# The low parts of 64 weight units of an encoder block, by an accumulating transfer in place of a subtraction

## The chip, the cores and the metric

The kernel runs on one core of a Trainium2 chip. The metric is the device time of one execution in microseconds (us). Before the change it is 1455.4 us, the median of three runs (1455.38 to 1455.77). The engines are named as in the profile: PE (TensorE, matrix products), PEld (its weight loads), DVE (VectorE), ACT (ScalarE), POOL (GpSimd) and SP (SyncE, which issues most DMAs).

## What is computed

One layer of a bidirectional encoder on 256 tokens of width 2048, in float32. Cut to what matters:

```python
h = rms_norm(x, attn_norm)
proj = h @ w_in                                  # q, k, v of two attention branches, and two gates
ya = windowed_gqa(qa, ka, va, table, sink)       # banded attention
yb = dilated_attention(qb, kb, vb, table)        # three dilations, merged
merged = sigmoid(ga) * (ya @ w_branch_a) + sigmoid(gb) * (yb @ w_branch_b)
x = x + merged @ w_out
hf = rms_norm(x, ffn_norm)
g = dwconv_centred(hf @ w_ffn_gate, conv_w, conv_b)
x = x + (gelu(g) * (hf @ w_ffn_up)) @ w_ffn_down # inner width 5632
x = x + sigmoid(rms_norm(x, ple_norm) @ w_ple_gate) * (p @ w_ple_proj)
out = rms_norm(x, final_norm)
```

## The kernel before

**Split products.** A float32 matrix product is made of three products of operands in the rounded type float32r. Each operand is split into a high part, its rounding, and a low part, the rest. `thirds` (L405 to L410) multiplies high by high (L408), high by low of the weights (L409) and low by high (L410), all into the same PSUM bank. The stages with 128-column moving weights do the same in `unit_blocks` (L335 to L358).

**Weights.** All weights come from HBM as 258 pieces of 128 partitions by 2048 columns, in the order in which they are used. SP loads a piece into one of three buffers `raw` (`load`, L250 to L258). `produce` (L285 to L311) makes one unit at a time, a part of a piece with at most 1024 columns: ACT writes the high part `hi` (L305), DVE writes the low part `lo` as the piece less `hi` (L306). Plain units (kind `n`) go to a ring of 6 buffers (tiles `uh`, `ul`), units of sums to a ring of 2 (`vh`, `vl`). Before a unit of piece p is made, the loads up to piece p + 2 are issued; a load must wait until the buffer's last readers have ended. When PE has used a unit for the last time, `drop` frees its place and `pump` makes what fits.

**Stages and pieces.** Stage A holds the projections for attention, with attention woven in. Behind it come the gates (B0 to B3), each followed by its share of the two branch products (ba, bb), then the output projection (D0, D1), and twice an up-projection (E0, E1) with two stages of the down-projection (F00, F01; F10, F11), the small projection pp, and the last gate G0, G2, G3. In the quad stages B, D, F and G0 (`quad_stage`) a piece holds two by two blocks of 512 columns. A piece of kind `S` or `Z` is multiplied in seven products by sums of blocks, each of three matmuls: it has two plain units and two units of sums, and DVE makes those sums in `raw` first (L282, L283, L295 to L297). A piece of kind `s` is multiplied in eight plain products and has two plain units. The branch products and G2, G3 have pieces of kind `w`, also two plain units and eight products (`wide_stage`). The kinds alternate in B and D (`SsSsSsSs`; B0 begins with four `s`), and in F (`ZZsZsZsZsZs`; `ZsZsZsZsZss` in the second half). For pieces of kind `Z` two of the sums are made ahead, in E0 and E1, by loads and stores on POOL's DMA queue (`sum_ahead`, L268 and L275, 52 of each), and loaded with the piece.

**Order.** Work beside the products is hung onto product numbers by `at` and done by `run_due`: gathers, norms, turns of rows into columns (L939, with roundings at L512, L513) and the ends of a stage (L890 to L894, L971 to L990, L1005, L1007). `keep` marks instructions that stay in program order. The rest is ordered on each engine by the framework's planner, so ACT's order can differ from the program's; each engine then takes its instructions strictly in turn.

Of the kernel before, what the change touches and what calls it, by code (L numbers as in the profile page):

```python
# [10 lines left out]
F32 = mybir.dt.float32  # L11
FR = mybir.dt.float32r
AF = mybir.ActivationFunctionType
ALU = mybir.AluOpType
# [149 lines left out]
_PIECES, _STAGES = _pieces()  # L164
# [3 lines left out]
def _unit_list():  # L168

    units, of = [], []  # L170
    for p, (kind, _) in enumerate(_PIECES):
        if p == 0:
            cuts = [("n", a * P, b * P) for a, b in ((0, 1), (1, 4), (4, 7), (7, 11), (11, PIECE))]
        elif kind == "Z":
            cuts = [("n", WIDE, 2 * WIDE), ("n", 2 * WIDE, 4 * WIDE), ("T21", 0, 2 * WIDE), ("T03", 2 * WIDE, 4 * WIDE)]
        elif kind == "S":
            cuts = [("n", 0, WIDE), ("n", 2 * WIDE, 4 * WIDE), ("T13", 0, 2 * WIDE), ("T24", 2 * WIDE, 4 * WIDE)]
        else:
            cuts = [("n", 0, 2 * WIDE), ("n", 2 * WIDE, 4 * WIDE)]
        of.append(list(range(len(units), len(units) + len(cuts))))  # L180
        units += [(p, *cut) for cut in cuts]
    return units, of


_UNITS, _UNITS_OF = _unit_list()
_FBLOCKS = [(u, o) for p, (kind, _) in enumerate(_PIECES) if kind == "f" for u in _UNITS_OF[p]
            for o in range((_UNITS[u][3] - _UNITS[u][2]) // P)]
_LAST_OF = {u: o for u, o in _FBLOCKS}
# [5 lines left out]
def _encoder(ctx: ExitStack, tc, xt, pt, xrow, cols, gainrow, table, onehot, mask, ident_in, wts, out):  # L194
    nc = tc.nc
# [12 lines left out]
    def bank(which, *shape):  # L208

        if which in RING:  # L210
            n = turns.get(which, 0)
            turns[which] = n + 1
            which = RING[which][n % len(RING[which])]
        else:
            which = BANK[which]
        return ps.tile(list(shape) or [P, 2 * T], F32, name="bank", tag="b%d" % which, bufs=1)
# [33 lines left out]
    def load(r, a=0, b=PIECE):  # L250
        if a == 0:
            raws[r] = wpool.tile([P, PIECE * P], F32, name="raw", bufs=3)
        if _PIECES[r][0] == "Z":
            nc.sync.dma_start(raws[r][:, WIDE:], wts[r][:, WIDE:])
            nc.sync.dma_start(raws[r][:, :WIDE], ahead.pop(r))
        else:
            nc.sync.dma_start(raws[r][:, a * P:b * P], wts[r][:, a * P:b * P])
        state["raw"] = r + 1  # L258
# [20 lines left out]
    def sums_of_weights(raw):  # L279

        q = [raw[:, i * WIDE:(i + 1) * WIDE] for i in range(4)]
        nc.vector.tensor_tensor(q[1], q[0], q[1], op=ALU.subtract)  # L282
        nc.vector.tensor_tensor(raw[:, 2 * WIDE:], raw[:, 2 * WIDE:], view(q[0], 0, (0, 2), (1, WIDE)), op=ALU.subtract)  # L283

    def produce():  # L285

        u = state["unit"]
        p, kind, a, b = _UNITS[u]
        while state["raw"] < min(p + 3, _NPIECES):
            load(state["raw"])  # L290
        raw = raws[p]
        ring = "u" if kind == "n" else "v"
        if kind == "T13":
            q = [raw[:, i * WIDE:(i + 1) * WIDE] for i in range(4)]
            nc.vector.tensor_tensor(raw[:, :2 * WIDE], raw[:, WIDE:3 * WIDE], raw[:, :2 * WIDE], op=ALU.subtract)  # L295
            nc.vector.tensor_tensor(q[2], q[2], q[0], op=ALU.subtract)
            nc.vector.tensor_tensor(q[3], q[3], q[2], op=ALU.subtract)  # L297
        behind = _PIECES[p][0] == "Z" == _PIECES[p - 1][0]
        if kind == "T21" and not behind:
            sums_of_weights(raw)  # L300
        src = raw[:, a:b]
        pool = wpool if ring == "u" else held["tok"]
        hi = pool.tile([P, b - a], FR, name=ring + "h", bufs=RINGS[ring])
        lo = pool.tile([P, b - a], FR, name=ring + "l", bufs=RINGS[ring])
        nc.scalar.activation(hi, src, AF.Copy)  # L305
        nc.vector.tensor_tensor(lo, src, hi.bitcast(F32), op=ALU.subtract)  # L306
        if behind and u == _UNITS_OF[p][1]:
            sums_of_weights(raw)
        made[u] = (hi, lo)
        state["unit"] = u + 1  # L310
        state[ring] -= 1  # L311

    def pump():
        while not state["early"] and state["unit"] < len(_UNITS):
            p, kind = _UNITS[state["unit"]][:2]
            if state["u" if kind == "n" else "v"] <= 0 or kind != "n" and "tok" not in held:
                break
            produce()

    def weights(u):  # L320
        while state["unit"] <= u:
            produce()
        return made[u]
# [167 lines left out]
    keep = tc.keep_in_program_order  # L491
# [148 lines left out]
    for step in order:  # L640
        if len(step) == 3:
            produce()
        else:
            for k in range(*step):
                gained(hs[:, k, :], x[:, k, :], gain(0, k))
            ready = step[1]
        while state["at"] < min(FIRST * ready, _EARLY[state["unit"]]):
            k, e = divmod(state["at"], FIRST)
            block(firsts[e], hs[:, k, :], k == 0, k == KC - 1)
        while 4 * done + 9 < state["at"] // FIRST:  # L650
            square(done)
            done += 1
# [16 lines left out]
    b = bank("misc", NH, 2 * T)  # L669
# [470 lines left out]
    for half in range(2):  # L1140
# [3 lines left out]
        stage = "E%d" % half  # L1144
# [87 lines left out]
    for t in range(2):  # L1232
        for h in range(2):
            cols = slice(3 * WIDE + h * T, 3 * WIDE + (h + 1) * T)
            u, r = c[t][:, WIDE + h * T:WIDE + (h + 1) * T], xr[:, t, cols]
# [72 lines left out]
```

## Time and profile before

The profiled execution has a span of 1453.7 us from its first instruction to its last; the median of the runs, 1455.4 us, lies 1.7 us above it. The mean granted TensorE clock is 0.997 of full speed.

| | |
|---|---|
| SP's loads of weights waiting for `ul` of DVE (L257) | 718.4 us in 148 waits, the longest 10.1 |
| ACT's high parts `uh` (L305) waiting for PE's L410 | 106.5 us in 78 waits |
| ACT's high parts `uh` waiting for a load of `raw` | 41.5 us in 35 waits |
| DVE's low parts `ul` (L306) waiting for ACT's `uh` | 65.9 us in 61 waits |
| DMA, main queue (SP): bytes, share of 16 engines | 280.46 MB, 53.1% |
| HBM read, written | 299.94 MB, 8.95 MB |

A row of the timeline gives the start and the duration of an instruction in us from the span's start, its engine, line and operation, what it writes and reads, and in brackets how long the engine was idle before it and what released it. Neighbours of one form are merged (x3). A matmul of 512 columns is shown with 0.39 us, though the next one starts earlier: matmuls overlap.

### The profile page before, as it was taken

The page shows a single profiled execution, that of the slowest core. Times are in us where ns is not written, and L with a number is a line of the kernel's source. Part 1 is how long each engine was busy: PE and PEld are TensorE (multiplying, and loading weights), DVE is VectorE, ACT ScalarE, POOL GpSimd, SP SyncE. Part 2 cuts the span into 40 slices and gives each one's busy share as a digit, 9 for nine tenths or more (in the row PEclk, how much of TensorE's full clock was granted, in tenths as well). Part 3 has the DMA queues.
Part 4 walks back from the last instruction along what each step waited for, and adds up shares of the span by engine and source line. Part 5 has one row for each costly group of instructions (what it writes and reads, how often), then busy time and mean ns, then how long its engine had stood idle before and what let it go on. Part 6 is the DMA issues. An engine that isn't in the chain of part 4 may idle for free.

```text
span 1453.7 us, 19747 instructions
## 1 busy us (share of the span) xinstructions
PE 1442.7 (99%) x7470; PEld 1234.0 (85%) x7470; DVE 1220.8 (84%) x1730; ACT 829.6 (57%) x1148; POOL 73.8 (5%) x113
## 2 busy tenths in 40 slices
PE   9999999999999999999999999999999999999997
PEld 8888888888888888888888888888888888888885
DVE  7677665679998989989877999997878799998994
ACT  7455544546555656566545566465545466555753
POOL 0000000000000000000221100000121200000000
PEclk9999999999999999999999999999999999999998
DMA  9753445435456456465767655566776765556462
GB/s 330 252 209 146 155 167 175 172 143 203 189 190 231 180 210 239 178 253 203 277 238 267 241 208 198 189 248 227 263 275 243 271 236 213 197 194 233 173 236 82
DMA packets 58522, 310.17 MB, mean 213 GB/s; under 512 B 7028, under 2 KB 12020, under 8 KB 29500
## 3 DMA queue, kind: packets, MB, share of 16 engines
q1 hardware_dynamic: 49388, 280.46, 53.1%
q0 software_dynamic: 8320, 27.27, 5.2%
q8 instruction: 58, 0.95, 0.3%
q10 hardware_dynamic: 720, 1.19, 0.2%
q14 instruction: 36, 0.29, 0.1%
HBM read 299.94 MB, written 8.95 MB: 212 GB/s over the span
## 4 chain that ended last, share of the span: by engine, by line
PE 98%; DMA 0%; issue 0%; DVE 0%; ACT 0%; SPq 0%; POOLq 0%; POOL 0%; DVEq 0%
PE bank L351 29%; PE bank L358 15%; PE bank L408 15%; PE bank L409 14%; PE bank L410 14%; PE bank L397 2%; PE bank L399 2%; PE bank L398 2%; PE bank L335 2%; PE bank L336 1%; PE bank L939 1%; PE bank L755 0%; PE bank L703 0%; PE bank L702 0%; PE bank L701 0%; DMA raw<-in_wts 0%
## 5 line engine op out<-in xcount | busy, mean ns | idle before, releaser
L305 ACT ACTIVATE uh<-raw 128x1024 fp32r<-128x1024 f32 (+2 forms) x519 | 518.1, 1010 | 297.0 <-PE bank L410 106.5
L306 DVE TENSOR_TENSOR ul<-raw,uh 128x1024 fp32r<-128x1024 f32 (+2 forms) x519 | 594.4, 1164 | 96.5 <-ACT uh L305 65.9
L351 PE MATMUL bank<-hf,uh 128*128 128x512 f32 x1408 | 336.3, 391 | 0.0
L351 PEld LDWEIGHTS bank<-hf,uh 128*128 128x128 f32 x1408 | 258.9, 188 | 50.1
L358 PEld LDWEIGHTS bank<-hf,ul 128*128 128x128 f32 x1408 | 180.4, 191 | 6.7
L358 PE MATMUL bank<-hf,ul 128*128 128x256 f32 x1408 | 182.8, 283 | 0.0
L305 ACT ACTIVATE vh<-raw 128x1024 fp32r<-128x1024 f32 x96 | 101.1, 1058 | 59.8 <-DVE raw L282 27.0
L306 DVE TENSOR_TENSOR vl<-raw,vh 128x1024 fp32r<-128x1024 f32 x96 | 116.3, 1220 | 1.1
L351 PE MATMUL bank<-hs,uh 128*128 128x512 f32 x432 | 103.6, 392 | 0.0
L351 PEld LDWEIGHTS bank<-hs,uh 128*128 128x128 f32 x432 | 79.5, 188 | 15.6
L410 PE MATMUL bank<-uh,act 128*128 128x512 f32 x218 | 84.9, 390 | 0.0
L409 PE MATMUL bank<-ul,act 128*128 128x512 f32 x218 | 84.8, 389 | 0.0
L408 PE MATMUL bank<-uh,act 128*128 128x512 f32 x218 | 84.6, 390 | 0.0
L496 ACT ACTIVATE t<-bank 128x256 f32<-128x256 f32 x122 | 45.3, 374 | 59.8 <-PE bank L358 48.7
L408 PE MATMUL bank<-uh,hs 128*128 128x512 f32 x172 | 67.4, 392 | 0.0
L410 PE MATMUL bank<-uh,hs 128*128 128x512 f32 x172 | 67.2, 391 | 0.0
L409 PE MATMUL bank<-ul,hs 128*128 128x512 f32 x172 | 67.0, 389 | 0.0
L1084 ACT ACTIVATE gw<-gw,cl 128x256 f32<-128x256 f32 x44 | 24.0, 594 | 72.2 <-DVE gw L1081 71.9
L271 DVE TENSOR_TENSOR ahead<-ahead 128x256 f32<-128x256 f32 x52 | 21.9, 422 | 46.8 <-DMA ahead<-in_wts 46.8
L268 POOL DMA_DIRECT2D ahead<-in_wts x52 | 39.0, 750 | 375.7 <-DMA ahead<-ahead 207.0
L358 PE MATMUL bank<-hs,ul 128*128 128x256 f32 x432 | 56.6, 284 | 0.0
L358 PEld LDWEIGHTS bank<-hs,ul 128*128 128x128 f32 x432 | 54.5, 191 | 1.0
(266 smaller groups left out, 2423.8 us busy)
## 6 DMA issues: line engine op xcount, KB each, us to landing
raw<-in_wts SPq DMA_DIRECT2D x225, 1024.0 KB, 4.9
ahead<-in_wts POOLq DMA_DIRECT2D x52, 384.0 KB, 5.2
raw<-in_wts SPq DMA_DIRECT2D x26, 768.0 KB, 5.1
ahead<-ahead POOLq DMA_DIRECT2D x52, 128.0 KB, 4.4
raw<-ahead SPq DMA_DIRECT2D x26, 256.0 KB, 4.9
raw<-in_wts SPq DMA_DIRECT2D x12, 512.0 KB, 7.0
xr<-in_xrow SPq DMA_DIRECT2D x4, 512.0 KB, 8.4
x<-in_xt SPq DMA_DIRECT2D x13, 128.0 KB, 6.0
```

Source lines behind the costliest of these rows:

```text
L268: keep(nc.gpsimd.dma_start(q, wts[p][:, :3 * WIDE].rearrange("p (q c) -> p q c", c=WIDE)[:, :, cols]))
L305: nc.scalar.activation(hi, src, AF.Copy)
L306: nc.vector.tensor_tensor(lo, src, hi.bitcast(F32), op=ALU.subtract)
L335: nc.tensor.matmul(acc, hi[:, w], m, start=first, stop=False, skip_group_check=True)
L351: nc.tensor.matmul(acc, weights(u)[0][:, o * P:(o + 1) * P], m, start=first, stop=False, skip_group_check=True)
L358: nc.tensor.matmul(acc[:, T:], weights(u)[1][:, o * P:(o + 1) * P], m[:, :T], start=False, stop=last, skip_group_check=True)
L397: nc.tensor.matmul(acc[:, :n * P], xh, hi, start=(k == 0), stop=False)
L398: nc.tensor.matmul(acc[:, :n * P], xh, lo, start=False, stop=False)
L408: nc.tensor.matmul(acc, sh, wh, start=first, stop=False)
L409: nc.tensor.matmul(acc, sh, wl, start=False, stop=False)
L410: nc.tensor.matmul(acc, sl, wh, start=False, stop=last)
L496: keep(nc.scalar.activation(t, acc[:, T:], AF.Copy, scale=scale))
```

## The change

For 64 plain units, the second unit of each piece of kind `s` or `w` in the stages B, ba, bb, D, F and G0 (the set `_MOVED`), the low part is no longer made by DVE. ACT first writes the negated rounding of the unit into `lo`, then the rounding into `hi`, and POOL's queue issues a DMA that adds the piece to `lo`, from `raw` in SBUF to `lo` in SBUF, 128 partitions by 1024 elements. `lo` then holds the piece less its rounding, as before, though not rounded again. The DMAs stay in program order. All other units are made as before.

```diff
+_MOVED = {_UNITS_OF[p][1] for stage in _STAGES if stage[0] in "BbDFG" and stage not in ("G2", "G3")
+          for p in _STAGES[stage] if _PIECES[p][0] in 'sw'}
...
         hi = pool.tile([P, b - a], FR, name=ring + "h", bufs=RINGS[ring])
         lo = pool.tile([P, b - a], FR, name=ring + "l", bufs=RINGS[ring])
-        nc.scalar.activation(hi, src, AF.Copy)
-        nc.vector.tensor_tensor(lo, src, hi.bitcast(F32), op=ALU.subtract)
+        if u in _MOVED:
+            nc.scalar.activation(lo, src, AF.Copy, scale=-1.0)
+            nc.scalar.activation(hi, src, AF.Copy)
+            keep(nc.gpsimd.dma_start(lo, src if _PIECES[p][0] in "sw" else wts[p][:, a:b], accum_op=ALU.add))
+        else:
+            nc.scalar.activation(hi, src, AF.Copy)
+            nc.vector.tensor_tensor(lo, src, hi.bitcast(F32), op=ALU.subtract)
         if behind and u == _UNITS_OF[p][1]:
             sums_of_weights(raw)
```

## The prediction

> **What bounds the kernel now.** I read the page first: the busy shares and the chain that ended last.
>
> ```profile
> span 1453.7 us, 19747 instructions
> ...
> PE 1442.7 (99%) x7470; PEld 1234.0 (85%) x7470; DVE 1220.8 (84%) x1730; ACT 829.6 (57%) x1148; POOL 73.8 (5%) x113
> ...
> PE 98%; DMA 0%; issue 0%; DVE 0%; ACT 0%; SPq 0%; POOLq 0%; POOL 0%; DVEq 0%
> ```
>
> PE is busy for 1442.7 of 1453.7 us and is 98% of the chain. A busy PE need not be a fast one, so I checked the spacing of its matmuls. The timeline shows the first and the last matmul of the two down-projection stages F00 and F01, and the chain in order of time shows a stretch in an up-projection.
>
> ```profile
> 874.64 0.40 PE L408 MATMUL bank<-vh,S 128*128 128x512 f32 x1
> ...
> 986.54 0.39 PE L410 MATMUL bank<-uh,act 128*128 128x512 f32 x1
> ```
> ```profile
> 640.55 3.65 PE bank L351 x16
> ```
>
> F00 and F01 hold 6 pieces of seven products and 5 pieces of eight each, every product three matmuls: 2 x (6 x 21 + 5 x 24) = 492. From the first start to the last, 111.90 us / 491 = 0.228 us, the same as 3.65 / 16 = 0.228 us in the undisturbed stretch. So PE runs at its pace through the stages that the change touches, although DVE is busy for 84% of the span. The list of waits of PE and of its weight loads (waiting line, releaser: us in total, times, longest) says how little is left:
>
> ```profile
> PE bank L336 <- DVE ul L306: 0.2, 1, 0.2
> ```
> ```profile
> PEld bank L408 <- ACT vh L305: 1.4, 4, 0.4
> PEld bank L939 <- DVE c L990: 1.1, 4, 0.3
> ...
> PEld bank L408 <- DVE c L988: 0.8, 3, 0.3
> ```
>
> Those three rows of weight loads, 1.4 + 1.1 + 0.8 = 3.3 us, are all that a quicker DVE could reach behind attention (I count ACT's vh among them, as it waits for DVE's sums). The change unloads an engine that PE hardly waits for. What matters is whether the new path is ever too late.
>
> **The change part by part.** It moves 64 units: the second halves of pieces of kind s and w, 6 + 3 x 4 in B0 to B3, 3 x 4 in the branch products, 8 in D, 5 + 5 + 6 + 6 in F, 4 in G0. Groups of instructions with their shapes apart, and the POOL issues there are now (min/median/max ns):
>
> ```profile
> L306 DVE TENSOR_TENSOR ul<-raw,uh 128x1024 fp32r<-128x1024 f32 x466 | 560.9, 1220 | 81.6 <-ACT uh L305 51.4 <-PE bank L358 15.5 <-issue 13.7
> L305 ACT ACTIVATE uh<-raw 128x1024 fp32r<-128x1024 f32 x466 | 486.0, 1054 | 236.0 <-PE bank L351 80.8 <-PE bank L410 71.8 <-DMA raw<-in_wts 39.1
> ```
> ```profile
> L268 POOL DMA_DIRECT2D ahead<-in_wts x52: 741/743/929, 638.8 to 1168.4; - x52
> ...
> DMA to landing us min/median/max: 3.3/5.2/6.3
> ```
>
> - Removed from DVE: 64 x 1.220 = 78.1 us. Added to ACT: 64 x 1.054 = 67.5 us. ACT is at 57%, so this hides beside PE as long as the units come early. Added to POOL: 64 issues of about 0.74 us = 47 us; behind attention POOL's queue holds besides only the small power operations of the norms, and the 52 loads and stores of sums ahead run in E0 and E1, while no moved unit is made. Each of these costs the end nothing by itself.
> - The low part now lands with a transfer from SBUF to SBUF that also adds; the trace of before has none. The nearest rows (KB, us from issue to landing, and what the queue's packets took):
>
> ```profile
> raw<-in_wts SPq DMA_DIRECT2D x225, 1024.0 KB, 4.9
> ahead<-in_wts POOLq DMA_DIRECT2D x52, 384.0 KB, 5.2
> ...
> ahead<-ahead POOLq DMA_DIRECT2D x52, 128.0 KB, 4.4
> ```
> ```profile
> q0 software_dynamic: 8320, 27.27, 5.2%
> ```
>
> POOL's queue moved 27.27 MB in 5.2% x 1453.7 = 75.6 us of all 16 engines, 0.361 MB/us. Of the 5.2 us, 384 KB (0.393 MB) are 1.1 us, of the 4.4 us, 128 KB are 0.4 us: both leave a fixed part of 4.1 us. The new transfer has 512 KB, 0.524 MB: 1.45 us if its bytes pass once, 2.9 us if reading the old contents counts like a second pass. So 5.55 to 7.0 us; I take the middle, 6.3 us, as I see no row that decides. It can start when the negated rounding is there, 1.05 us after the unit's first ACT instruction begins. The low part is therefore ready 6.6, **7.35** or 8.05 us after ACT's start; DVE's path takes 3.0 us in the steady rows below (422.61 + 1.22 - 420.82). The Trainium skill's page "DMA: Bandwidth & Descriptors", section "Anatomy of one DMA — SWDGE (gpsimd) path", fits 2.0 us plus bytes / 436e3 per us: 3.2 us for 512 KB as an estimate, hence ready after 4.25 us and nowhere late. The rows above stand against it (its fit gives 2.3 and 2.9 us where 4.4 and 5.2 were measured), and the measurements decide.
>
> Now what time there is. A steady place, a piece of eight in B2 (rows of ACT, DVE, PE):
>
> ```profile
> 420.82 1.04 ACT L305 ACTIVATE uh<-raw 128x1024 fp32r<-128x1024 f32 x1
> ```
> ```profile
> 422.61 1.22 DVE L306 TENSOR_TENSOR ul<-raw,uh 128x1024 fp32r<-128x1024 f32 x1
> ```
> ```profile
> 431.44 0.39 PE L409 MATMUL bank<-ul,hs 128*128 128x512 f32 x1
> ```
>
> From ACT's start to PE's first use of the low part: 10.62 us; 7.35 us fits. I worked this interval out for all 64; most have 8 to 13 us. Five are shorter than 7.35 us, all soon behind a stage's boundary: two in F01, of which I show the shorter, and one each in F11, D1 and F00 (in this order; ACT's rows, then PE's first use):
>
> ```profile
> 944.21 1.06 ACT L305 ACTIVATE vh<-raw 128x1024 fp32r<-128x1024 f32 x1 [7.03 <-DVE raw L282]
> ...
> 947.07 2.51 ACT L305 ACTIVATE uh<-raw 128x1024 fp32r<-128x1024 f32 x3
> ```
> ```profile
> 951.63 0.39 PE L409 MATMUL bank<-ul,act 128*128 128x512 f32 x1
> ```
> ```profile
> 1308.24 1.07 ACT L305 ACTIVATE uh<-raw 128x1024 fp32r<-128x1024 f32 x1 [0.61 <-PE bank L410]
> ...
> 1310.16 2.51 ACT L305 ACTIVATE uh<-raw 128x1024 fp32r<-128x1024 f32 x3
> ```
> ```profile
> 1315.70 0.39 PE L409 MATMUL bank<-ul,act 128*128 128x512 f32 x1
> ```
> ```profile
> 603.81 1.06 ACT L305 ACTIVATE uh<-raw 128x1024 fp32r<-128x1024 f32 x1 [1.06 <-PE bank L410]
> ...
> 606.07 1.05 ACT L305 ACTIVATE uh<-raw 128x1024 fp32r<-128x1024 f32 x1
> ```
> ```profile
> 612.37 0.39 PE L409 MATMUL bank<-ul,merged 128*128 128x512 f32 x1
> ```
> ```profile
> 886.71 1.06 ACT L305 ACTIVATE vh<-raw 128x1024 fp32r<-128x1024 f32 x1 [4.72 <-DVE raw L282]
> 887.67 1.04 ACT L305 ACTIVATE uh<-raw 128x1024 fp32r<-128x1024 f32 x1
> 888.62 1.04 ACT L305 ACTIVATE vh<-raw 128x1024 fp32r<-128x1024 f32 x1
> 889.57 2.52 ACT L305 ACTIVATE uh<-raw 128x1024 fp32r<-128x1024 f32 x3
> ```
> ```profile
> 895.54 0.39 PE L409 MATMUL bank<-ul,act 128*128 128x512 f32 x1
> ```
>
> In each the last ACT row begins with the moved unit. In F01 and F00 ACT had waited for DVE (7.03 and 4.72 us, for sums that stood behind a backlog), and one moved subtraction of 1.22 us is gone from that backlog, so ACT starts that much earlier. In F11 and D1 ACT had waited for PE to free a buffer, and nothing is won.
> F01: 951.63 - 947.07 = 4.56, + 1.22 = 5.78; short by 1.57. F11: 5.54; short by 1.81. D1: 6.30; short by 1.05. F00: 5.97 + 1.22 = 7.19; short by 0.16. A later unit of the same stage is made no later by PE's stall, so a stage pays its largest shortfall only. Sum 4.6 us. With a transfer of 5.55 us the same working gives 0.82 + 1.06 + 0.30 + 0 = 2.2 us, with 7.0 us 2.27 + 2.51 + 1.75 + 0.86 = 7.4 us.
> - What DVE's relief gives back: of the 3.3 us I take 1 us (the rows that name DVE itself hold 1.9).
> - The hi rounding of a moved unit comes behind the negated one, 1.05 us later; it is needed only one matmul (0.23 us) ahead of the low part, so the low part is later in all cases.
> - The raw buffer. Three pieces stand in SBUF, and SP's next load waits until the last reader of a buffer has ended: so far DVE, now the transfer, and all loads queued on SP behind it wait too. In B2:
>
> ```profile
> 423.86 0.33 SPq L257 DMA_DIRECT2D raw<-in_wts  x1
> ```
> ```profile
> 436.02 0.63 ACT L305 ACTIVATE uh<-raw 128x512 fp32r<-128x512 f32 x1 [1.08 <-PE bank L410]
> ...
> 441.42 1.06 ACT L305 ACTIVATE uh<-raw 128x1024 fp32r<-128x1024 f32 x1 [0.45 <-PE bank L410]
> ```
>
> The load goes out as DVE's row above ends (422.61 + 1.22). Now it goes out at 420.82 + 7.35 = 428.2 and lands 4.9 us later at 433.1; ACT turns to that piece at 436.02. This covers 2.9 us more, so the cost is nothing.
>
> Sum: 4.6 - 1 = 3.6 us. The profiled execution has a span of 1453.7 us, and the median of the runs, 1455.4 us, lies 1.7 us above it; I add to the median: 1459.0 us, slower by 0.25%. The bounds of the transfer give 1456.6 and 1461.8. About 0.2% (2.9 us) is what a measurement of this kernel can tell from no change, so the lower end of this case counts as the same.
>
> **The rivals.**
> *All hidden, no change.* If the transfers land like the quickest of the 384 KB ones, 3.3 us plus 0.4 us for the larger size, the low part is ready after 4.8 us, and only F11 and F01 are near (5.54 and 5.78 us, both enough). Against it stands the median of 5.2 us; for it, that the planner which orders each engine's instructions (ACT's four rows in F00 run vh, uh, vh, uh, where the program makes both vh first) may give the slow units more room. Time 1455.4 less up to 1 us, or up to 2.9 us more if a stall or two stay.
> *Faster.* With 78.1 us less on DVE, the catching up behind D0, F00 and F10 is over sooner, and all 3.3 us of weight-load waits go: 1452.1 us. It decides only if no transfer is late. For more than that PE has no idle time to give.
> *The buffers' cycle becomes the bound.* A moved unit frees a buffer, the buffer takes the next seven-product piece, and behind it comes the next moved unit but one, two pairs of pieces later: 1.05 us, the transfer, 4.9 us of load and 441.42 - 436.02 = 5.4 us of ACT. PE takes 2 x 45 x 0.228 = 20.5 us for the two pairs, so it decides from a transfer of 9.1 us on, beyond the 6.3 us that the slowest row has. If the adding transfers took 10 us beside the weights' loads, each of some 32 cycles would lose 0.9 us: 29 us, less what the slack at the start absorbs, say 1470 to 1484.
> The Trainium skill's page "SBUF — State Buffer", section "SBUF: two separate sides", warns that VectorE in a two-port mode holds up GpSimd's descriptors. The POOL row above spreads only from 741 to 929 ns with DVE busy; a hold of one DVE instruction more would be an estimated 1 us on the transfer, within the bounds taken.
>
> **How the numbers follow.** Late units behind the boundaries, the forecast: 0.46, of which 0.08 stays under 2.9 us. All hidden: 0.39. The cycle: 0.09. Faster by more than 2.9 us: 0.06. So slower 0.38 + 0.09 = 0.47, same 0.39 + 0.08 = 0.47, faster 0.06. The range leaves out most of the faster case and the cycle: 1453.8 to 1466, the upper end above 1461.8 for a transfer held up by the loads beside it.
>
> **What would show it.** L306 has 64 fewer instructions, L305's or the new line's negations 64 more, DVE is down by some 78 us and ACT up by some 67. The new issue stands in the DMA list with 512 KB; its time to landing decides: below 5 us all hidden, 5.5 to 7 us the forecast, above 9 us the cycle. PE's waits would name this transfer, in F01, F11 and D1 with 1 to 2 us each; in B, nothing. I am wrong if PE waits for it in B's steady pieces, or if the waits of SP's loads push ACT's starts behind PE's need.

## The result and the profile after

The changed kernel takes 1561.8 us, the median of four runs (1558.77 to 1571.61), beside 1455.39 us of four runs of the kernel before (1455.22 to 1455.77). The ratio is 1.0743, with a 95% interval from 1.0711 to 1.0776: slower by 7.4%, 106 us. The profiled execution took 1563.53 us, its span is 1561.7 us and its mean granted TensorE clock 0.982 (0.997 before).

The page of the kernel after: its span, the busy time of the engines and the engines of the chain that ended last.

```profile
span 1561.7 us, 20020 instructions
...
PE 1473.2 (94%) x7470; PEld 1246.1 (80%) x7470; DVE 1158.4 (74%) x1666; ACT 884.3 (57%) x1212; POOL 129.1 (8%) x177
...
PE 61%; DMA 23%; issue 7%; DVE 6%; ACT 3%; SPq 0%; POOLq 0%; POOL 0%; ACTq 0%; DVEq 0%
```

The groups of the subtractions that DVE kept and of the negations that ACT got:

```profile
L313 DVE TENSOR_TENSOR ul<-raw,uh 128x1024 fp32r<-128x1024 f32 x402 | 484.6, 1219 | 157.2 <-ACT uh L312 127.6 <-PE bank L365 15.6 <-issue 13.3
```
```profile
L308 ACT ACTIVATE ul<-raw 128x1024 fp32r<-128x1024 f32 x64 | 67.1, 1048 | 7.9 <-PE bank L416 5.3 <-PE bank L365 2.6
```

64 subtractions of 128 x 1024 are gone, 560.9 - 484.6 = 76 us by the group, and 62 us of DVE's busy time, where overlapping instructions count once. ACT has 67.1 us more by the group, POOL is up by 55. None of it buys anything: PE has the same 7470 matmuls, and transfers now hold 23% of the chain. By the two pages of the profile PE's idle time rose from 11.0 to 88.5 us and its busy time by 30.5 us; together these are the 108.0 us by which the two spans differ. The transfer itself, in the list of DMAs with the main loads, and the spread of its time from issue to landing:

```profile
raw<-in_wts SPq DMA_DIRECT2D x225, 1024.0 KB, 5.4
ul<-raw POOLq DMA_DIRECT2D x64, 512.0 KB, 7.6
```
```profile
L310 POOL DMA_DIRECT2D ul<-raw x64: 847/867/1051, 294.5 to 1494.0; - x64
...
DMA to landing us min/median/max: 4.5/7.6/12.1
```

The median is 7.6 us, but it is not one time with some scatter: the quickest land in 4.5 us, a quarter need 9.0 us or more. The issue times in the trace tell the two apart: 21 of the 64 have a weight load issued within 0.6 us of them, and these land after 8.2 to 12.1 us (median 9.2); the other 43 take 4.5 to 9.7 us (median 6.2). Who waits for it (PE, its weight loads, ACT and SP; line, releaser, us in total, times, longest):

```profile
PE bank L416 <- DMA ul<-raw: 59.2, 25, 5.8
```
```profile
PEld bank L416 <- DMA ul<-raw: 70.3, 27, 6.2
```
```profile
ACT uh L312 <- DMA raw<-in_wts: 172.9, 77, 5.4
```
```profile
SPq L259 <- DVE ul L313: 531.8, 100, 9.5
SPq L259 <- DMA ul<-raw: 333.2, 48, 12.7
SPq L259 <- DVE vl L313: 183.7, 36, 11.0
SPq L256 <- DMA ul<-raw: 115.7, 16, 9.6
```

PE and its weight loads wait for mostly the same transfers, so their rows are not added. SP's loads now wait for all 64 transfers (48 + 16), and ACT finds the weights late in 77 places for 172.9 us, where it was 35 places and 41.5 us.

Where the time went: from the first to the last matmul of each stage, in us, before and after.

| stage | before | after | | stage | before | after |
|---|---|---|---|---|---|---|
| B0 | 46.2 | 49.8 | | D1 | 43.6 | 55.4 |
| B1 | 41.6 | 54.6 | | F00 | 55.8 | 61.9 |
| B2 | 41.8 | 49.6 | | F01 | 55.9 | 67.8 |
| B3 | 41.8 | 52.4 | | F10 | 56.2 | 64.8 |
| D0 | 41.7 | 54.0 | | F11 | 57.7 | 64.8 |
| | | | | G0 | 40.6 | 45.7 |

These are 97.9 us; bb0 to bb2 add 3.2, 2.7 and 1.8: 105.6 us in all. Every stage with alternating kinds of pieces pays, and not only near its start: the longest stalls of B1, B3 and D0 begin 41 to 43 us behind the stage's first matmul. ba0 to ba3, G2 and G3 keep their times within 0.6 us.

One cycle in B2 shows how. The rows are PE's, then SP's and POOL's issues, then ACT's and DVE's, then PE's again; a bracket tells the idle time before an instruction and what ended it.

```profile
444.00 0.50 PE L416 MATMUL bank<-ul,yb 128*128 128x512 f32 x1 [2.34 <-DMA ul<-raw]
```
```profile
444.08 0.33 SPq L259 DMA_DIRECT2D raw<-in_wts  x1
...
446.14 0.33 SPq L259 DMA_DIRECT2D raw<-in_wts  x1
...
454.36 0.33 SPq L259 DMA_DIRECT2D raw<-in_wts  x1
```
```profile
444.31 0.86 POOL L310 DMA_DIRECT2D ul<-raw  x1 [8.93 <-DVE ul L313]
```
```profile
442.86 1.04 ACT L308 ACTIVATE ul<-raw 128x1024 fp32r<-128x1024 f32 x1
...
450.28 1.58 ACT L312 ACTIVATE uh<-raw 128x512 fp32r<-128x512 f32 x2 [4.48 <-DMA raw<-in_wts]
455.33 1.06 ACT L312 ACTIVATE uh<-raw 128x1024 fp32r<-128x1024 f32 x1 [3.47 <-DMA raw<-in_wts]
```
```profile
450.94 0.69 DVE L313 TENSOR_TENSOR ul<-raw,uh 128x512 fp32r<-128x512 f32 x1 [3.51 <-ACT uh L312]
451.67 1.23 DVE L297 TENSOR_TENSOR raw<-raw 128x1024 f32<-128x1024 f32 x1
452.81 1.22 DVE L313 TENSOR_TENSOR ul<-raw,uh 128x1024 fp32r<-128x1024 f32 x1
453.95 0.68 DVE L995 SCALAR_TENSOR_TENSOR c<-c,bank 128x512 f32<-128x512 f32 x1
```
```profile
454.68 0.80 PE L415 MATMUL bank<-vh,S 128*128 128x512 f32 x1 [3.21 <-DVE c L995]
```

The transfer of an earlier moved unit lands just before 444.00: PE, idle for 2.34 us, goes on, and at 444.08 SP issues the load that had waited for the same buffer. At that time the next moved unit has just been negated (442.86 + 1.04 = 443.90), so its transfer is issued at 444.31, behind a load of 1 MB and beside a second one from 446.14 on. (POOL's bracket names DVE, whose subtraction ended at 444.22; the two transfers named below also go out 0.41 us after the end of their negation.) It lands at 454.30, 9.99 us after its issue, and the second load at 455.22, 9.1 us after its own. The pieces come late, so ACT sits idle for 4.48 and 3.47 us, DVE behind it for 3.51 us, and a PSUM eviction (L995) stands in DVE's queue behind the late low parts: PE waits 3.21 us for it. At 454.36, 0.06 us after the landing, the next withheld load goes out. Here the round does not go on: the next two transfers, at 463.64 and 471.58, find the load ahead of them nearly done (it lands 1.75 and 1.60 us after their issue) and land after 4.56 and 4.70 us.

So a transfer can hold back a load that then meets the next transfer, but that is the smaller part of the collisions. Of the 21 loads that were issued within 0.6 us of a transfer, 7 had last waited for the landing of an earlier transfer, as at 444.08; 13 had waited for a low part that DVE makes from a seven-product piece (`vl`), and one for another instruction of DVE.

A second loss hides in a busy PE. The timeline of PE in an earlier stall:

```profile
416.86 0.39 PE L417 MATMUL bank<-uh,hs 128*128 128x512 f32 x1
417.09 0.39 PE L415 MATMUL bank<-uh,hs 128*128 128x512 f32 x1
422.62 0.80 PE L416 MATMUL bank<-ul,hs 128*128 128x512 f32 x1 [5.14 <-DMA ul<-raw]
423.21 0.63 PE L417 MATMUL bank<-uh,hs 128*128 128x512 f32 x1
423.64 0.63 PE L415 MATMUL bank<-uh,hs 128*128 128x512 f32 x1
```

Matmuls that started 0.23 us apart start 0.59 and 0.43 us apart after the stall: the granted clock has gone to 0.50. The trace has ten such stretches of 3.4 or 6.8 us, 51.2 us in all; before there was none until the last 10 us. PE stands idle in 7.8 us of them, so they lose about half of the other 43.4 us, some 22 us of the 106. In this trace the clock fell at all five stalls of 4.0 us and more, and at five of the ten of 2.4 to 3.3 us. The Trainium skill's page "TensorE: Matmul & The Clock Gate", section "Part 1: The HAM clock gate", states that the array falls to half its rate after an idle window of about 3.4 us and comes back after as long a busy one. The lengths of the stretches and the spacing of 0.43 us agree with that; the stalls of less than 3.4 us that were followed by half clock (the shortest 2.4 us) do not.

The same 250 us of both spans, before and then after (us, PE, PEld, DVE, ACT and POOL busy, clock, DMA share, GB/s), show the load on the DMA engines:

```profile
310.00:560.00 250.00, 250.00 (x1127) 206.01 (x1126) 234.22 (x294) 148.83 (x170) 0.00 (x0) 1.00 0.51 190
```
```profile
310.00:560.00 250.00, 219.60 (x950) 175.66 (x948) 172.26 (x222) 144.36 (x167) 21.71 (x25) 0.97 0.75 213
```

### The profile page after: what moved, and what is told of

It reads as the page before. It is cut to its first block, busy times and chain, and to the rows that moved or that the text cites. A ratio compares the mean times of both kernels' runs of the same rounds, so it can differ in the third digit from the quotient of the medians.

```text
span 1561.7 us, 20020 instructions
## 1 busy us (share of the span) xinstructions
PE 1473.2 (94%) x7470; PEld 1246.1 (80%) x7470; DVE 1158.4 (74%) x1666; ACT 884.3 (57%) x1212; POOL 129.1 (8%) x177
## 3 DMA queue, kind: packets, MB, share of 16 engines
q0 software_dynamic: 17536, 60.83, 16.1%
## 4 chain that ended last, share of the span: by engine, by line
PE 61%; DMA 23%; issue 7%; DVE 6%; ACT 3%; SPq 0%; POOLq 0%; POOL 0%; ACTq 0%; DVEq 0%
PE bank L358 26%; PE bank L365 14%; DMA raw<-in_wts 13%; DMA ul<-raw 10%; PE bank L416 4%; PE bank L417 4%; PE bank L415 4%; DVE vl L313 2%; PE bank L404 2%; DVE ul L313 2%; PE bank L406 2%; PE bank L405 2%; PE bank L342 1%; ACT vh L312 1%; ACT uh L312 1%
## 5 line engine op out<-in xcount | busy, mean ns | idle before, releaser
L313 DVE TENSOR_TENSOR ul<-raw,uh 128x1024 fp32r<-128x1024 f32 (+2 forms) x455 | 520.2, 1156 | 216.8 <-ACT uh L312 186.8
L312 ACT ACTIVATE uh<-raw 128x1024 fp32r<-128x1024 f32 (+2 forms) x455 | 450.4, 1004 | 361.3 <-DMA raw<-in_wts 172.9
L310 POOL DMA_DIRECT2D ul<-raw x64 | 55.7, 871 | 974.3 <-ACT ul L308 502.3
L416 PE MATMUL bank<-ul,act 128*128 128x512 f32 x218 | 88.9, 408 | 19.9 <-DMA ul<-raw 19.9
L417 PE MATMUL bank<-uh,act 128*128 128x512 f32 x218 | 87.4, 402 | 0.0
L415 PE MATMUL bank<-uh,act 128*128 128x512 f32 x218 | 86.5, 400 | 0.0
L308 ACT ACTIVATE ul<-raw 128x1024 fp32r<-128x1024 f32 x64 | 67.1, 1048 | 7.9 <-PE bank L416 5.3
L416 PEld LDWEIGHTS bank<-ul,act 128*128 128x128 f32 x218 | 42.6, 195 | 33.7 <-DMA ul<-raw 24.9
L415 PE MATMUL bank<-uh,hs 128*128 128x512 f32 x172 | 69.1, 401 | 0.0
L417 PE MATMUL bank<-uh,hs 128*128 128x512 f32 x172 | 68.8, 401 | 0.0
L309 ACT ACTIVATE uh<-raw 128x1024 fp32r<-128x1024 f32 x64 | 66.9, 1045 | 2.4 <-PE bank L358 2.4
```

The costliest lines, as they stand in the source:

```text
L308: nc.scalar.activation(lo, src, AF.Copy, scale=-1.0)
L310: keep(nc.gpsimd.dma_start(lo, src if _PIECES[p][0] in "sw" else wts[p][:, a:b], accum_op=ALU.add))
L415: nc.tensor.matmul(acc, sh, wh, start=first, stop=False)
L416: nc.tensor.matmul(acc, sh, wl, start=False, stop=False)
L417: nc.tensor.matmul(acc, sl, wh, start=False, stop=last)
```

## The experiments

Theory R: the transfer holds the raw buffer, SP's next load is late, and loads and transfers close into a cycle. Theory L: the low part is simply too late for PE. Theory B: the transfers' traffic slows the loads. Theory A: ACT's 64 added instructions, and the planner's new order, delay the units. Each experiment but the last is a single run, beside the kernel before on the same chip, which took 1455.75 us for the first four (one run), 1456.46 for the next four (one run) and 1455.31 for the last four (the median of thirteen). Edits are shown against the changed kernel, cut to what matters; a new line with a transfer takes the place of the old one.

**ACT's work alone.** DVE makes the low part again, over the negated rounding:

```diff
-            keep(nc.gpsimd.dma_start(lo, src if ..., accum_op=ALU.add))
+            nc.vector.tensor_tensor(lo, src, hi.bitcast(F32), op=ALU.subtract)
```

> No transfers: ACT writes the negated rounding into the low part's buffer and then the high part, and DVE makes the low part as before the change. Only ACT's 64 extra instructions (about 67 us of ACT) and the planner's new order are left. Theory A (ACT's extra work or the order that it brings makes units late) expects a good part of the 106 us, 1480 us or more. The buffer theory R, the late-part theory L and the traffic theory B all expect 1455 to 1459 us.

Measured: 1456.55 us, 0.8 us more. A falls: the 64 negations cost nothing that can be told from no change.

**The addend from HBM.** The raw buffer is no longer read by the transfer:

```diff
+            keep(nc.gpsimd.dma_start(lo, wts[p][:, a:b], accum_op=ALU.add))
```

> As the changed kernel, but the adding transfer reads the piece from HBM and not from its buffer, so the buffer is free as soon as ACT and DVE have read it; the low part still comes by the transfer, and HBM reads 33.5 MB more. Theory R (the transfer holds the piece's buffer, SP's next load goes out late, and round this cycle ACT, PE and the loads follow each other) expects most of the 106 us gone, 1460 to 1485 us, and SP's waits for the transfer gone. Theory L (the low part by itself comes too late for PE) expects 1540 us or more. Theory B (the transfers slow the loads of weights) expects 1560 us or more, as the traffic grows.

Measured: 1553.82 us, 98 us more. The DMA list and the waits of the weight loads:

```profile
ul<-in_wts POOLq DMA_DIRECT2D x64, 512.0 KB, 9.3
```
```profile
PEld bank L416 <- DMA ul<-in_wts: 67.4, 28, 7.0
```

SP no longer waits for a transfer, and yet the time is nearly the same. R alone doesn't carry the loss. With the loads free to go at once, 55 of the 64 transfers have a load issued within 0.6 us of them, where it was 21; they land later (9.3 us), and PE waits for them as before.

**Held, not needed (two tries).** DVE makes the low part, and a transfer that nobody needs adds the piece into HBM scratch, from `raw` (first) or from HBM (second); four transfers that fill the scratch at the start are left out here:

```diff
-            keep(nc.gpsimd.dma_start(lo, src if ..., accum_op=ALU.add))
+            nc.vector.tensor_tensor(lo, src, hi.bitcast(F32), op=ALU.subtract)
+            keep(nc.gpsimd.dma_start(spill[...], src, accum_op=ALU.add))          # first
+            keep(nc.gpsimd.dma_start(spill[...], wts[p][:, a:b], accum_op=ALU.add)) # second
```

> DVE makes all low parts as before the change (ACT writes the negated rounding as well); the transfer still reads the piece's buffer and adds it into a scratch place in HBM that nobody reads. So the buffer is held and the traffic is there, but PE waits for no transfer. Theory R expects nearly the whole loss: 1530 us or more. Theory L expects 1455 to 1465 us. Theory B expects a good part of the loss too, and e4 tells it from R.

> As the run before, but the transfer reads the piece from HBM: nothing is held and nothing waits, only the traffic of 64 adding transfers is left (512 KB each, into HBM). Theory B expects 1500 us or more. Theories R and L expect 1455 to 1465 us.

Measured: 1481.94 and 1534.82 us. Neither tells what it was to tell. In the first the transfer no longer waited for ACT's negation and went out as soon as the piece had landed, so it held the buffer for a shorter time than in the change. In the second it waited for nothing at all, and many of the 64 ran in the first stages, where they fought with the first loads (POOL and PE in 40 slices of the span):

```profile
PE   8993999999999999999999998999999998999997
...
POOL 0122200000000000000222210000222221000000
```

Both were set up anew.

**The buffer held, alone.** The negation goes into the first half of `raw` (once its readers are done), DVE makes the low part, and the transfer adds within the buffer:

```diff
-            nc.scalar.activation(lo, src, AF.Copy, scale=-1.0)
+            nc.scalar.activation(raw[:, :b - a], src, AF.Copy, scale=-1.0)
...
+            nc.vector.tensor_tensor(lo, src, hi.bitcast(F32), op=ALU.subtract)
+            keep(nc.gpsimd.dma_start(raw[:, :b - a], src, accum_op=ALU.add))
```

> DVE makes all low parts as before the change. In the 64 moved units ACT writes the negated rounding over the first half of the piece's buffer, whose unit has been made by then, and the same transfer (512 KB, SBUF to SBUF, adding) goes onto it: same start, same traffic, the buffer is held, and PE waits for no transfer. Theory R (the held buffer and the cycle of loads) expects 1530 us or more. Theory L (the low part itself comes too late) expects 1455 to 1470 us. If both halves are needed for the loss, it lies between.

Measured: 1564.0 us, 108 us more. The waits of SP, of ACT and of PE:

```profile
SPq L259 <- DMA raw<-raw: 348.4, 47, 11.2
```
```profile
ACT uh L313 <- DMA raw<-in_wts: 219.6, 94, 6.0
```
```profile
PE bank L416 <- DVE c L996: 29.0, 9, 6.6
PE bank L947 <- DVE xr L1013: 9.9, 2, 8.5
```

Nobody needs the transfer's result, and the loss is whole. PE waits for evictions that stand in DVE's queue behind low parts whose weights came late. One reservation: the negation here also waits for the first unit's readers, so the buffer may be held a little longer than in the change.

**The late part, alone.** The addend is the high part of the unit before, so that nothing of `raw` is held:

```diff
+            keep(nc.gpsimd.dma_start(lo, made[u - 1][0].bitcast(F32), accum_op=ALU.add))
```

> The low part comes by the same adding transfer from SBUF, but its source is the high part of the piece's first unit and not the piece's buffer (so the low part has other values: this leaves out the right low part of 64 units). The buffer is free when ACT has read it, PE still waits for the transfer. Theory L expects 1530 us or more. Theory R expects 1455 to 1470 us. In between: both count.

Measured: 1553.42 us, 97 us more, with the picture of the addend from HBM though it reads no HBM:

```profile
ul<-uh POOLq DMA_DIRECT2D x64, 512.0 KB, 9.1
```
```profile
PEld bank L416 <- DMA ul<-uh: 70.6, 25, 7.4
```

So each suffices without the other, 108 and 97 us, and both together cost 106: they don't add up. Neither run is simply the change less one part, though: with the buffer free, 53 of the 64 transfers have a load issued within 0.6 us of them, where it is 21 in the change and 24 in the run with the buffer held, and they land after 9.1 us instead of 7.6. What both share is the adding transfer beside the loads.

**A plain copy.** The transfer copies instead of adding:

```diff
+            keep(nc.gpsimd.dma_start(lo, src))
```

> As the changed kernel, but the transfer copies the piece into the low part and does not add (the low part of 64 units has other values, the difference is left out). A packet of 4096 bytes should then take about 159 ns, not 327, and a transfer that meets no load about 3.2 us, not 4.5. Every theory that lives on the transfer's length (R and L) expects a loss well under the 106 us, 1460 to 1500 us. If the fixed part or the held buffer at any length counts, 1520 us or more.

Measured: 1485.51 us, 29 us more. The same bytes over the same queue, with the same buffer held, and over two thirds of the loss gone (the DMA list, then the queue's share of 16 engines):

```profile
ul<-raw POOLq DMA_DIRECT2D x64, 512.0 KB, 4.9
```
```profile
q0 software_dynamic: 17536, 60.83, 11.5%
```

In the changed kernel this queue took 16.1% of 1561.7 us, in the kernel before 75.6 us. So an adding transfer takes (251.4 - 75.6) / 64 = 2.75 us of all 16 engines, a copying one (170.6 - 75.6) / 64 = 1.48 us. The transfers' packets of 4 KB say the same: 328 and 174 ns in the median (I had expected 159 for the copy).

**Every second moved unit.**

```diff
+_MOVED = set(sorted(_MOVED)[::2])
```

> The change for 32 of the 64 units, every second one in order. If each late unit costs by itself, about half of the loss, 1505 to 1515 us. If the loss comes from transfers that meet each other and the loads, or from the closed cycle from one moved unit to the next but one, clearly less than half: 1456 to 1490 us.

Measured: 1494.58 us, 38 us more; the transfers land after 5.5 us in the median. Half of them cost less than half (53 us): 8 of the 32, where it was 21 of 64, have a load issued within 0.6 us of them.

**The traffic alone, again.** DVE makes the low part; a transfer as large, from the high part in SBUF, adds into HBM scratch as soon as the high part is there, holds no raw buffer, and nobody waits for it:

```diff
+            nc.vector.tensor_tensor(lo, src, hi.bitcast(F32), op=ALU.subtract)
+            keep(nc.gpsimd.dma_start(spill[...], hi.bitcast(F32), accum_op=ALU.add))
```

> The traffic by itself, better than in e4: DVE makes all low parts, and a transfer of 512 KB for each of the 64 units adds the unit's finished high part (SBUF) into a scratch place in HBM that nobody reads. It goes out when the high part is there, so it lies where the changed kernel's transfers lie; it holds no piece's buffer, and PE waits for none. Theory B (the transfers slow the loads of weights) expects 1490 us or more. If only the held buffer and the late part count, 1456 to 1465 us.

Measured: 1486.91 us, 32 us more, with ACT waiting for the loads:

```profile
ACT uh L314 <- DMA raw<-in_wts: 112.1, 66, 5.5
```

So the traffic by itself, so placed, gives about 30% of the loss. It is no upper bound on what the traffic costs in the change: these transfers went out behind the high part, only 6 of the 64 had a load issued within 0.6 us of them, and they ended in HBM and not in SBUF.

**A copy with the buffer free.**

```diff
+            keep(nc.gpsimd.dma_start(lo, made[u - 1][0].bitcast(F32)))
```

> As e6 (source is the high part of the piece's first unit, the buffer is free), and the transfer copies and does not add (the right low part of 64 units is left out). If lateness against each unit's interval is the measure, a copy that stands behind a load lands after about 6.5 to 7 us, 8 to 8.5 us after ACT's start, later than PE's first use in some ten units only: 1460 to 1475 us. If PE is held up in other ways, it stays above 1485 us like e7.

Measured: 1500.55 us, 45 us more, 15 us worse than the copy that holds the buffer, where I had expected it to be better:

```profile
ul<-uh POOLq DMA_DIRECT2D x64, 512.0 KB, 6.4
```

The freed buffer lets SP's load go at once, and it meets the transfer, in 53 of 64 cases instead of 20: 6.4 us to landing instead of 4.9. Holding the buffer back keeps some loads out of the transfer's way.

**Half the width.** Only 512 of the 1024 columns take the new path, the others stay with DVE:

```diff
+            m = (b - a) // 2
+            nc.scalar.activation(lo[:, m:], src[:, m:], AF.Copy, scale=-1.0)
...
+            nc.vector.tensor_tensor(lo[:, :m], src[:, :m], hi[:, :m].bitcast(F32), op=ALU.subtract)
+            keep(nc.gpsimd.dma_start(lo[:, m:], src[:, m:], accum_op=ALU.add))
```

> The change for the second half (512 columns) of each of the 64 units; DVE makes the low part of the first half. The transfer has 256 KB: alone about 3.2 us, beside a load 6 to 8 us. By the length of the transfer as the measure it lies near the plain copy (e7, which lost 29 us): 1475 to 1500 us. If each transfer costs a fixed amount whatever its length, 1540 us or more.

Measured: 1489.62 us, 34 us more, at 5.1 us to landing (median). Half the bytes cost a third.

**Eight units with much time.**

```diff
+_MOVED &= {102, 104, 106, 122, 152, 182, 212, 360}
```

The expectation misstates the places: three of the eight are in B0, one in each of ba0 to ba3, and one in F00.

> The change for 8 of the 64 units only, all with at least 12 us between ACT's start and PE's first use, and far apart (four in B0, one in each but the last of the branch products' pairs, one in F00), so that no cycle of moved units can close. A transfer that lands within 10.5 us is in time here. Expected by both theories: 1454.5 to 1457.5 us, no change. If single transfers cost by delaying loads, 1460 us or more.

Measured: 1456.26 us in ten runs (1455.15 to 1458.68), the kernel before 1455.31 in thirteen; ratio 1.0007, 0.9997 to 1.0016: no change.

```profile
ul<-raw POOLq DMA_DIRECT2D x8, 512.0 KB, 6.1
```

No matmul and no weight load waits for these transfers, though the slowest took 8.9 us. An adding transfer costs nothing where PE needs its low part 12 us or more after ACT's start and the moved units are few; it also saves nothing. No version beats the kernel before.

## Why the prediction was wrong

- *PE bounds it, and DVE's relief can give at most 3.3 us*: not contradicted. The kernel with eight units moved, where nothing is late, is no faster, but it takes only eight subtractions from DVE; no run takes all 64 without a late transfer.
- *ACT's and POOL's added work hides beside PE*: held for ACT, by the run with ACT's work alone; for POOL's issues only the run with eight units speaks. A POOL issue took 0.87 us, not 0.74.
- *The transfer takes 5.55 to 7.0 us, the middle 6.3*: here the sum began to fail. Both bounds asked only what the transfer's own bytes cost on top of a fixed part of 4.1 us, taken from the medians of other transfers. Alone it took 4.5 us, below the lower bound: less its 2.75 us on the engines that leaves about 1.7 us, so the 4.1 us were too much for a fixed part. With a load issued within 0.6 us it took 8.2 to 12.1 us, above the upper bound. The idea that an added byte counts like two passes was near (2.75 against 1.48 us of 16 engines) and belonged into the load on the DMA engines, which rose from 0.51 to 0.75.
- *Ready 7.35 us after ACT's start*: POOL issues the transfer 0.4 us after the negation, so at the median it is 1.04 + 0.4 + 7.6 = 9.0 us, and in the cycle shown 454.30 - 442.86 = 11.4 us. Most of the 64 units had 8 to 13 us.
- *A stage pays its largest shortfall only; in B, nothing*: failed. That holds if a stall leaves the transfers as they are. Here later transfers of the same stage collide anew, and B1 to B3 pay 13.0, 7.8 and 10.6 us. PE waiting for the transfer in B was the prediction's own sign of being wrong.
- *The raw buffer: 2.9 us to spare, so nothing*: failed, and with it the whole of ACT's lateness. It took the transfer at 6.3 us and the load at 4.9 us, as if the one did not meet the other; in the cycle shown they took 9.99 and 9.1 us. ACT's waits for loads went from 41.5 to 172.9 us, and the run with the buffer held, and the low part from DVE, lost 108 us.
- *The rival of the buffers' cycle*: right in part. SP's loads did wait for the transfers, 448.9 us in 64 waits, and the load did come late for ACT; but most of the colliding loads had waited for DVE and not for a transfer, so the cycle is not the whole mechanism, and it was priced too low. I let it decide from a transfer of 9.1 us on and compared that with 6.3 us, the slowest of the 384 KB loads, though 15 of the 64 transfers reach it. In the cycle shown, the moved unit after next is negated at 470.11, 27.25 us after 442.86, where PE needs 20.5 us for two pairs; I had priced 0.9 us a cycle for transfers of 10 us. Some 3 of these 6.75 us are the half clock from 453.72 to 460.55.
- *The clock*: not thought of. A sum that prices stalls at their length leaves out the half clock behind them, here some 22 us.

What the runs leave open: how much of the 106 us belongs to the held buffer and how much to the late part, as each alone gives nearly the whole and each run also changes how often transfers meet loads (in the changed kernel itself, 59.2 us of PE's idle time ended with a late transfer); why a transfer takes its first packet so late beside a load; from which length of a stall on the clock falls; and what share the planner's other order has in the changed kernel (it puts some negations behind the high part), beyond what the run with ACT's work alone excludes.

## What to carry to other kernels

The time of a transfer that isn't in the trace is bounded beside the transfers that it will meet, not only by its own bytes: see which queued loads are issued at about the same time, whether a reader elsewhere or an earlier transfer releases them. Where the transfer can meet a load anew in each turn, a stall in one stage does not pay for the later ones, so such a cost is counted per turn and not once per stage. Where PE is 98% of the chain and waits for nothing, relieving another engine can win only the few waits that name it, while any new path carries its whole risk.

## What the runs showed of the hardware

- An adding transfer from SBUF to SBUF takes about 328 ns for each packet of 4 KB, a copying one 174 ns (medians, changed kernel and plain copy).
- The adding transfer's first packet came 1.4 to 1.6 us after the issue when it was alone. It came 4.6 to 5.2 us after it in the 16 cases that had a weight load issued within 0.6 us and no earlier transfer under way. In the cycle shown the load's packets went first, and the second load, issued 1.83 us behind the transfer, shared the engines with it. Of 16 copying transfers in the same place nine waited 4.2 to 4.8 us for their first packet, where a lone one waits 1.1. The trace does not show why.
- Adding transfers of half the size and copying ones of full size both leave POOL's queue at 11.5% of the 16 engines, half as many adding ones at 11.2%; they cost 34, 29 and 38 us. Among the kernels that hold the buffer the loss goes with the time on the DMA engines, not with the number of transfers.
- In the changed kernel 3.4 or 6.8 us at half clock came with each of five stalls of PE of 4.0 us and more, and with five of the ten of 2.4 to 3.3 us.
